# A hybrid decoder step: attention of all superblocks first, then the feed-forward over three equal segments by seven-product (Strassen) multiplication

## The chip, the cores and the metric

The kernel runs on one core of a Trainium2 chip. A core has five engines that run side by side and wait for each other by semaphores: TensorE (PE, matrix products; its weight loads are shown apart as PEld), VectorE (DVE), ScalarE (ACT), GpSimd (POOL) and SyncE (SP), which here only issues transfers. SBUF is the on-chip memory of 128 partitions, PSUM the accumulators of PE in eight banks of 512 columns, DRAM the memory outside. The metric is the device time of one launch in microseconds (us); less is better.

## The reference

One layer of a decoder is computed for 2048 prompt tokens and for 64 sample tokens (8 sequences of 8), with weights in common, in float32. For the prompt:

```
h = rmsnorm(x) * g_mix;  q, k, v, u = split(h @ w_in)          # 1024 -> 512, 128, 128, 512
a = window attention(q, k, v)      # 8 heads, window 128, ALiBi, one sink a head
p = pooling mixer(u)               # means over 2, 4, 8, 16 tokens minus u, @ w_pool, * pool_scale
x = x + concat(a, p) @ w_out
h = rmsnorm(x) * g_cross;  s = (h @ w_cq) . mem_k
x = x + (softmax(s / 16) @ mem_v) @ w_co                       # 4 heads, 256 memory tokens
h = rmsnorm(x) * g_ffn
x = x + relu(h @ w_up)**2 @ w_down                             # 1024 -> 4096 -> 1024
y = rmsnorm(x) * g_final
```

The sample tokens go the same way with caches of keys, values, pooling inputs and memory. The outputs are y, the last keys, values and pooling inputs of both groups, and the memory's keys and values.

## The kernel before, in words

**Number format.** Every large product is made of three: each operand is split in a rounded part "hi" (ACT casts) and the rest "lo" (DVE subtracts), and PE adds hi x hi, hi x lo and lo x hi (`mm3`, lines 111 to 113, and `dense`, lines 280 to 282). Weights are split too: `Stream.emit` takes two slots of `WS` (12 slots of 128x1024) and one raw buffer of `FS` (6), loads 512 KB (L131), casts (L132) and subtracts (L133). `Stream.items` is a fixed list in the order of use; `pump` runs ahead as long as slots and raw buffers are free and fewer than five tiles are ready, with `resW` and `resF` keeping some back.

**Order of work.** The tokens lie in three superblocks of two blocks each (384 + 384, 384 + 384, 256 + 320 with the sample tokens). A prologue computes the memory's keys and values and folds them with w_cq and w_co into the matrices `a_s` and `b_s` in DRAM; w_pool is folded into the lower half of w_out (`wo_s`). Then `superblock(s)` runs all stages of one superblock before the next one begins:

- input projection (10 chunks of 128 output columns by 2 blocks) mixed with the window attention, whose scratch lies in the buffers `XT` of x;
- output stage: 8 chunks by 2 blocks; each result is added to x in `XT` (`add_evac`, L884), squared and summed for the norm (`Norm.sq`, L205 and L206);
- cross stage: two halves of two heads; each half takes four tiles of `a_s` at once and goes over the 128-token tiles of both blocks (24 matmuls of 512 columns a tile);
- B stage: 8 chunks of `b_s` by 2 blocks (`add_evac2`, L1085), then the norm and the split into the feed-forward's input `h3` (`Norm.apply`, L232, 233 and 235);
- feed-forward: eight groups of 512 hidden columns. `up(g)` makes four chunks by two blocks of 24 matmuls; `up_evac` does relu on ACT, the square on POOL (L1123), the cast on ACT (L1125) and the rest on DVE (L1126). `down(g - 1)` makes 4 tiles by 2 blocks by 2 halves of 12 matmuls, each added to x by DVE (L1156). The next superblock's x is loaded and normed (`norm1`) beside the last two down groups; `final` makes the final norm and stores y.

**What sets the order of the queues.** The program is unrolled, tiles carry their dependences, and a scheduler puts the instructions of each engine in an order at build time; each engine then works through its queue in that order. `later` and `flush` hold generators that emit deferred work (norms) between chunks. All transfers are issued by SP.

Each weight of the feed-forward is loaded and split once a superblock, three times in all.

## Time and profile before

| what | us |
|---|---|
| median of 3 runs (2638.29 to 2641.51) | 2640.59 |
| profiled execution: listed by its span | 2639.7 |
| PE busy | 2565.7 |
| DVE busy | 1302.4 |
| ACT busy | 984.2 |
| POOL busy | 680.7 |
| splits of weights on DVE (L133, 330 of them) | 422.8 |
| casts of weights on ACT (L132, 330 of them) | 346.9 |

The page gives the profiled execution's span, from its first to its last instruction; no other time of that execution is listed, and the span stands 0.9 us under the median of the runs. A line that starts with L and a number is that line of the kernel. In rows of groups, "out<-in" names the tiles with their numbers left out (`w` weight slots, `f` raw buffers, `mm` and `aux` PSUM, `act` activations, `t` scratch, `x` the residual), then come the count, the busy time, the mean duration, and the idle time of the engine just before them with what ended it. In stretches of the span each engine has its busy time and its count of instructions; the last three columns are the clock granted to PE as a share of full speed, the busy share of the 16 DMA engines, and GB/s. Durations of neighbouring matmuls overlap, so their cost is the distance of their starts.

### The profile page before, as it was taken

To read this page: it belongs to the slowest core of one execution; us is meant where nothing else is said; L and a number is where in the kernel's file an instruction comes from. 1 tells how busy PE (TensorE), PEld (TensorE's weight loads), DVE (VectorE), ACT (ScalarE), POOL (GpSimd) and SP (SyncE) were. 2 spreads that over 40 slices of the span, in tenths; PEclk is the share of its full clock that TensorE was granted. 3 is DMA by queue.
4 is the path that set the end of the run, shared out by engine and by line. 5 is a ranking of instruction groups with operands and counts; after the bars stand their busy time and mean duration, and the time that the engine had idled before them with its cause. 6 is when DMAs were issued, how large, how long until landed. Compare 5 with 4: busy or idle time off the path is not lost. (4 is left out here: it accounts for less than half of the span.)

```text
span 2639.7 us, 39195 instructions
## 1 busy us (share of the span) xinstructions
PE 2565.7 (97%) x15725; PEld 2458.0 (93%) x15725; DVE 1302.4 (49%) x2276; ACT 984.2 (37%) x1923; POOL 680.7 (26%) x730
## 2 busy tenths in 40 slices
PE   7899999999999999999999999999999999999998
PEld 7798979999999999997999999999999669999998
DVE  7568453633333357936363333334766646334334
ACT  6666342422222244834342222223355434332231
POOL 3215322411111153433241111113334214111111
PEclk9999999999999999999999999999999999999999
DMA  7843212211111123131111111112414473222210
GB/s 261 260 130 101 72 49 74 71 64 63 61 62 64 56 72 113 45 132 56 65 58 63 65 64 64 65 56 71 140 60 149 176 266 112 87 80 81 88 57 37
DMA packets 92251, 244.76 MB, mean 93 GB/s; under 512 B 16740, under 2 KB 31524, under 8 KB 90916
## 3 DMA queue, kind: packets, MB, share of 16 engines
q1 hardware_dynamic: 92068, 242.25, 26.9%
q8 instruction: 123, 2.02, 0.3%
q14 instruction: 60, 0.49, 0.1%
HBM read 219.53 MB, written 22.69 MB: 92 GB/s over the span
## 5 line engine op out<-in xcount | busy, mean ns | idle before, releaser
L281 PE MATMUL mm<-act,w 128*128 128x384 f32 (+2 forms) x2784 | 899.1, 323 | 6.5 <-DVE act L235 5.0
L280 PE MATMUL mm<-act,w 128*128 128x384 f32 (+2 forms) x2784 | 902.8, 324 | 2.5 <-ACT act L623 1.6
L282 PE MATMUL mm<-act,w 128*128 128x384 f32 (+2 forms) x2784 | 897.4, 322 | 1.1 <-DVE w L133 0.9
L132 ACT CAST w<-f 128x1024 fp32r<-128x1024 f32 x330 | 346.9, 1052 | 737.4 <-PE mm L112 453.9
L133 DVE TENSOR_TENSOR w<-f,w 128x1024 fp32r<-128x1024 f32 x330 | 422.8, 1286 | 317.9 <-ACT w L132 312.0
L111 PE MATMUL mm<-act,w 128*128 128x384 f32 (+2 forms) x1728 | 554.1, 321 | 13.6 <-ACT act L372 8.3
L112 PE MATMUL mm<-act,w 128*128 128x384 f32 (+2 forms) x1728 | 550.3, 318 | 0.0
L113 PE MATMUL mm<-act,w 128*128 128x384 f32 (+2 forms) x1728 | 549.8, 318 | 0.0
L281 PEld LDWEIGHTS mm<-act,w 128*128 128x128 f32 x2784 | 527.3, 189 | 16.3 <-DVE act L235 6.7
L280 PEld LDWEIGHTS mm<-act,w 128*128 128x128 f32 x2784 | 527.4, 189 | 7.2 <-issue 2.3
L282 PEld LDWEIGHTS mm<-act,w 128*128 128x128 f32 x2784 | 527.3, 189 | 1.8 <-DVE w L133 1.6
L1123 POOL TENSOR_TENSOR t<-t 128x384 f32<-128x384 f32 (+2 forms) x192 | 219.0, 1141 | 1034.8 <-ACT t L1122 1034.8
L1156 DVE TENSOR_TENSOR x<-mm,x 128x384 f32<-128x384 f32 (+2 forms) x384 | 199.7, 523 | 326.5 <-PE mm L113 326.5
L111 PEld LDWEIGHTS mm<-act,w 128*128 128x128 f32 x1728 | 328.6, 190 | 15.8 <-ACT act L372 8.3
L112 PEld LDWEIGHTS mm<-act,w 128*128 128x128 f32 x1728 | 328.3, 190 | 1.2 <-DVE act L373 0.2
L113 PEld LDWEIGHTS mm<-act,w 128*128 128x128 f32 x1728 | 328.4, 190 | 0.1
L206 POOL TENSOR_TENSOR t<-t,t 128x384 f32<-128x384 f32 (+2 forms) x168 | 203.0, 1209 | 348.9 <-ACT t L205 331.4
L1126 DVE TENSOR_TENSOR act<-t,act 128x384 fp32r<-128x384 f32 (+2 forms) x192 | 103.2, 537 | 300.4 <-ACT act L1125 300.4
L1125 ACT CAST act<-t 128x384 fp32r<-128x384 f32 (+2 forms) x192 | 93.8, 488 | 237.5 <-POOL t L1123 237.5
L1122 ACT ACTIVATE t<-mm 128x384 f32<-128x384 f32 (+2 forms) x192 | 88.2, 459 | 95.2 <-PE mm L282 94.2
L205 ACT ACTIVATE t<-x 128x384 f32<-128x384 f32 (+2 forms) x140 | 68.4, 499 | 145.4 <-DVE x L1085 64.9
L111 PE MATMUL mm<-w,act 128*128 128x512 f32 x288 | 116.7, 406 | 3.2 <-ACT f L330 1.7
(184 smaller groups left out, 2199.0 us busy)
## 6 DMA issues: line engine op xcount, KB each, us to landing
f<-in_wup SPq DMA_DIRECT2D x96, 512.0 KB, 3.5
f<-in_wdn SPq DMA_DIRECT2D x96, 512.0 KB, 3.5
f<-in_win SPq DMA_DIRECT2D x30, 512.0 KB, 3.6
f<-a_s SPq DMA_DIRECT2D x24, 512.0 KB, 3.2
f<-b_s SPq DMA_DIRECT2D x24, 512.0 KB, 4.2
x<-in_x SPq DMA_DIRECT2D x6, 1536.0 KB, 7.1
f<-in_wco SPq DMA_DIRECT2D x16, 512.0 KB, 4.9
f<-in_cmk SPq DMA_DIRECT2D x16, 512.0 KB, 4.5
```

Source lines behind the costliest of these rows:

```text
L111: nc.tensor.matmul(ps, Wh(k), Hh(k), start=first and i == 0, stop=False)
L112: nc.tensor.matmul(ps, Wh(k), Hl(k), start=False, stop=False)
L113: nc.tensor.matmul(ps, Wl(k), Hh(k), start=False, stop=final and i == last)
L132: nc.scalar.copy(th[:], r[:, 0:1024])
L133: eng.tensor_tensor(tl[:], r[:, 0:1024], f32(th[:]), ALU.subtract)
L206: nc.gpsimd.tensor_tensor(self.acc[:, 0:n], self.acc[:, 0:n], t[:, 0:n], ALU.add)
L280: nc.tensor.matmul(ps[:, 0:n], w8(th)[:, k, :], hi(b, k), start=k == 0, stop=False)
L281: nc.tensor.matmul(ps[:, 0:n], w8(th)[:, k, :], lo(b, k), start=False, stop=False)
L282: nc.tensor.matmul(ps[:, 0:n], w8(tl)[:, k, :], hi(b, k), start=False, stop=k == 7)
L1123: nc.gpsimd.tensor_tensor(q[:, 0:n], r[:, 0:n], r[:, 0:n], ALU.mult)
L1126: nc.vector.tensor_tensor(lo, q[:, 0:n], f32(hi), ALU.subtract)
L1156: nc.vector.tensor_tensor(bl.x(m), ps[:, 0:n], bl.x(m), ALU.add)
```

## The change

**Order.** `superblock(s)` now ends with the B stage. The residual x goes to `xq` and the normed input of the feed-forward to `hq`, both in DRAM. The next superblock's norm is loaded and squared in the second half of the cross stage, and applied in the B stage. After the third superblock, `mlp` goes over all 2112 tokens in three segments of 704, each with a left and a right half of 352 columns.

**Products.** A group of up has its weight (1024 x 512) in 2 x 2 blocks and the input in 2 x 2 blocks; instead of eight block products seven are made, in a form of Strassen's scheme. The seven combinations of the input are made once a segment (`xprep`, POOL sums, ACT casts, DVE subtractions), 14 slots of `ACTS`. The results are combined when they are emptied from PSUM (`ups`). Down groups 0 to 6 do the same (`downs`), with the input's combinations made from the hidden values in place (`hsplit`, two pairs of slots in turn), and with the outputs accumulated in combined form in x and in two extra accumulators, which `mid` undoes in the last of them. Down group 7 stays plain (`down_last`), and so does the final norm.

**Weight sums.** The combinations of the weights are made once, by `Work`: 60 jobs of load, five sums of 128x256 on DVE, store to `us_s` or `ds_s`; one step of it is run after each output chunk and each cross tile (`prep`), with two buffers in turn. The untouched block of each group is copied within DRAM, as are w_in, the upper half of w_out and the last group of w_down.

**Buffers.** `WS` has 10 slots instead of 12, but the window attention's keys (4 slots) move to a new shared tile "mc". Weights that were stored by the kernel, and w_in and w_out from superblock 1 on, are loaded straight into their lo slot; only `ext` items have a raw buffer. PSUM is grouped in four tiles of two banks for `mlp`.

The host's side lays x out by superblock and reads y by segment. The core of the diff:

```diff
         def emit(self):
-            key, raw, eng = self.items.popleft()
+            key, raw, eng, ext = self.items.popleft()
             th, tl = WS.get(), WS.get()
-            r = FS.get()
+            r = FS.get() if ext else f32(tl[:])
...
     for s in range(3):
         for c in CIN:
-            S.add(("in", s, c), io["win"][c])
+            S.add(("in", s, c), win_s[c] if s else io["win"][c], ext=s == 0)
...
+    for j in range(NSEG):
         for g in range(9):
...
+            if g < 8:
+                for i in ORD:
+                    S.add(("us", j, g, i), us_s[g, WIX[i]])
+            if 0 < g < 8:
+                for i in ORD:
+                    S.add(("ds", j, g - 1, i), ds_s[g - 1, WIX[i]], eng=nc.gpsimd if i in (5, 1) else None)
+            if g == 8:
+                for c in range(4):
+                    S.add(("dn", j, c), dn_s[c])
...
-        kz = [[WS.get() for _ in range(2)] for _ in range(2)]
+        kzt = mc_tile(F32R)
+        kz = [[kzt[:, 896 * (2 * kv + hl):896 * (2 * kv + hl) + 896] for hl in range(2)] for kv in range(2)]
...
             nc.vector.tensor_tensor(bl.x(c), ps[:, 0:bl.n], bl.x(c), ALU.add)
             bl.norm.sq(c)
+            prep(s)
...
                         flush()
+                        prep(s)
+                        if hf == 1 and nxt is not None:
+                            x = len(sqs)
+                            for k in range(4):
+                                if x + k < 16:
+                                    nxt[(x + k) // 8].nm.sq((x + k) % 8)
+                                    sqs.append(1)
...
+        def after_co(b):
+            bl = blks[b]
+            for hf in range(2):
+                ACTS.put(*bl.pt[hf])
+            keep(xq, bl)
+            bl.norm.fin()
+            yield
+            for k in range(8):
+                nc.vector.scalar_tensor_tensor(bl.x(k), bl.x(k), vec[:, V_GFFN + k:V_GFFN + k + 1], bl.norm.r[:, 0:bl.n], ALU.mult, ALU.mult)
+                if k % 4 == 3:
+                    yield
+            TS.put(bl.norm.r)
+            keep(hq, bl)
...
+        def ups(j, g):
+            c11, c12, c21, c22 = Rv(g, 0, 0), Rv(g, 1, 0), Rv(g, 0, 1), Rv(g, 1, 1)
+            sm = {}
+            for i in ORD:
+                th, tl = S.next(("us", j, g, i))
+                while i not in Xc:
+                    flush()
+                Hh, Hl = Xc[i]
+                d = DD.get()
+                for q in range(2):
+                    mm3(d[:, 512 * q:512 * q + nh], range(4), lambda k: th[:, 512 * q + P * k:512 * q + P * k + P], lambda k: tl[:, 512 * q + P * k:512 * q + P * k + P],
+                        lambda k: Hh[:, nh * k:nh * k + nh], lambda k: Hl[:, nh * k:nh * k + nh])
+                WS.put(th, tl)
+                v = v2(d)
+                if i in (2, 5):
+                    t = sm[i] = TD.get()
+                    nc.scalar.copy(w2(t), v)
+                if i == 4:
+                    nc.vector.tensor_tensor(c21, v, w2(sm[2]), ALU.add)
+                    sm[4] = d
+                    relu2(c21)
...
+        def hsplit(g, i, dst):
+            X11, X21, X12, X22 = R(g, 0, 0, 2), R(g, 0, 2, 2), R(g, 1, 0, 2), R(g, 1, 2, 2)
+            pre = {4: (X21, X11, ALU.subtract), 3: (X12, X22, ALU.subtract), 1: (X11, X22, ALU.add),
+                   7: (X21, X11, ALU.add), 6: (X12, X11, ALU.add)}.get(i)
+            if pre:
+                nc.gpsimd.tensor_tensor(pre[0], pre[0], pre[1], pre[2])
+            src = {2: X11, 5: X22, 4: X21, 3: X12, 1: X11, 7: X21, 6: X12}[i]
+            hi, lo = dst[:, 0:2 * nh], dst[:, 2 * nh:4 * nh]
+            nc.scalar.copy(hi, src)
+            nc.vector.tensor_tensor(lo, src, f32(hi), ALU.subtract)
+            return hi, lo
...
+            make(0)
+            make(1)
+            for x, i in enumerate(ORD):
+                th, tl = S.next(("ds", j, g, i))
+                Hh, Hl = hc[x]
+                for pp in range(2):
+                    d = DD.get()
+                    for q in range(2):
+                        p = 2 * pp + q
+                        mm3(d[:, 512 * q:512 * q + nh], range(2), lambda k: th[:, 256 * p + P * k:256 * p + P * k + P], lambda k: tl[:, 256 * p + P * k:256 * p + P * k + P],
+                            lambda k: Hh[:, nh * k:nh * k + nh], lambda k: Hl[:, nh * k:nh * k + nh])
+                    if i in (4, 5):
+                        if g == 0:
+                            nc.scalar.copy(mac(i, pp), v2(d))
+                        else:
+                            nc.vector.tensor_tensor(mac(i, pp), v2(d), mac(i, pp), ALU.add)
+                    else:
+                        for e in (7, 6) if i == 1 else (i,):
+                            r = role(*M[e], pp)
+                            nc.vector.tensor_tensor(r, v2(d), r, ALU.add)
+                    DD.put(d)
+                    flush()
+                WS.put(th, tl)
+                if mid is not None:
+                    mid(i)
+                make(x + 2)
...
+        def step(self, load=True):
+            done = self.summed
+            self.summed = []
+            for x, t in self.loaded:
+                self.sums(t)
+                self.summed.append((x, t))
+            self.loaded = []
+            for x, t in done:
+                self.store(x, t)
+                self.bufs.append(t)
+            if load and self.jobs and self.bufs:
+                x, t = self.jobs.pop(0), self.bufs.pop(0)
+                self.load(x, t)
+                self.loaded.append((x, t))
...
+        def sums(self, t):
+            b = [t[:, 256 * i:256 * i + 256] for i in range(6)]
+            for d, a, c, op in ((4, 2, 3, ALU.add), (5, 0, 1, ALU.add), (2, 2, 0, ALU.subtract), (1, 1, 3, ALU.subtract), (0, 0, 3, ALU.add)):
+                nc.vector.tensor_tensor(b[d], b[a], b[c], op)
```

581 lines of the change are left out of this document (441 added, 140 removed).

## The prediction

> **What bounds the kernel now.** The page comes first. Its header and its line of busy time:
>
> ```profile
> span 2639.7 us, 39195 instructions
> ...
> PE 2565.7 (97%) x15725; PEld 2458.0 (93%) x15725; DVE 1302.4 (49%) x2276; ACT 984.2 (37%) x1923; POOL 680.7 (26%) x730
> ```
>
> PE has work 97% of the span, and 74.0 us are idle. Busy time alone doesn't show that PE is at its peak, so I next read the busy time by stretches: the start, the output stage and the cross stage of superblock 0, a stretch of its feed-forward, and the feed-forward of superblock 2.
>
> ```profile
> core 0: us, PE busy (x) PEld busy (x) DVE busy (x) ACT busy (x) POOL busy (x), PEclk, DMA share, GB/s
> 0.00:17.00 17.00, 8.27 (x50) 7.83 (x50) 7.54 (x15) 11.58 (x22) 4.76 (x10) 1.00 0.84 309
> 240.00:312.00 72.00, 70.01 (x392) 68.83 (x391) 28.02 (x38) 22.60 (x36) 28.41 (x28) 0.98 0.36 125
> 312.00:385.00 73.00, 69.82 (x329) 57.38 (x328) 45.88 (x75) 31.62 (x74) 23.81 (x29) 1.00 0.16 51
> 600.00:800.00 200.00, 200.00 (x1156) 200.00 (x1155) 68.90 (x96) 48.49 (x73) 27.69 (x24) 1.00 0.19 64
> 2240.00:2610.00 370.00, 370.00 (x2769) 370.00 (x2768) 145.22 (x231) 103.56 (x175) 62.77 (x61) 1.00 0.21 72
> ```
>
> In the feed-forward PE never pauses and DVE is busy 34% of the time (68.90 of 200). So the time of this part is the number of matmuls by the spacing of their starts. The timeline of PE gives the spacing for 384, 256 and 320 columns (the rows are three matmuls apart):
>
> ```profile
> 800.30 0.33 PE L280 MATMUL mm<-act,w 128*128 128x384 f32 x1
> ...
> 800.82 0.33 PE L280 MATMUL mm<-act,w 128*128 128x384 f32 x1
> ```
> ```profile
> 2299.90 0.28 PE L280 MATMUL mm<-act,w 128*128 128x256 f32 x1
> ...
> 2300.26 0.31 PE L280 MATMUL mm<-act,w 128*128 128x320 f32 x1
> ...
> 2300.70 0.31 PE L280 MATMUL mm<-act,w 128*128 128x320 f32 x1
> ```
>
> 0.52/3 = 0.1733 us, 0.36/3 = 0.1200 us and 0.44/3 = 0.1467 us. Halfway between 320 and 384 columns lies the new width of 352: 0.1600 us.
>
> **The matmuls removed.** Before, up and down take 32 tiles x 24 matmuls each, per block: 3072 of 384 columns in each of superblocks 0 and 1 (532.5 us each), and 1536 of 256 and 1536 of 320 columns in superblock 2 (409.6 us): 1474.5 us. After, a segment has 8 up groups of 7 products of 24 matmuls, 7 down groups of the same, and a plain last group of 2 x 4 x 24: 1344 + 1176 + 192 = 2712. Three segments are 8136 matmuls, 1301.8 us. **PE: -172.7 us.** All of it lies where PE sets the end, so it is gained in full if the seven products can be fed and emptied.
>
> The Trainium skill, "TensorE: Matmul & The Clock Gate", section Back-to-back issue gap, gives N/2.4 + 2.5 ns for an isolated matmul, by which the saving would be 160.8 us, an estimate; this trace has 173 ns at 384 columns where that formula has 162.5, and the rows above stay in the sum.
>
> **Weights without a raw buffer.** The six raw buffers of the stream go; a stored tile is now loaded straight into its "lo" slot. So its transfer can't start before PE has let go of the slot, and transfer, cast and split stand in a row behind that.
>
> ```profile
> f<-a_s SPq DMA_DIRECT2D x24, 512.0 KB, 3.2
> f<-b_s SPq DMA_DIRECT2D x24, 512.0 KB, 4.2
> ```
> ```profile
> L132 ACT CAST w<-f 128x1024 fp32r<-128x1024 f32 x330 | 346.9, 1052 | 737.4 <-PE mm L112 453.9 <-PE mm L281 237.5 <-issue 8.1
> L1125 ACT CAST act<-t 128x384 fp32r<-128x384 f32 x128 | 65.9, 515 | 164.0 <-POOL t L1123 164.0
> ```
> ```profile
> L133 DVE TENSOR_TENSOR w<-f,w 128x1024 fp32r<-128x1024 f32 x330 | 422.8, 1286 | 317.9 <-ACT w L132 312.0 <-PE mm L113 5.5
> L1156 DVE TENSOR_TENSOR x<-mm,x 128x384 f32<-128x384 f32 x256 | 141.5, 556 | 233.6 <-PE mm L113 233.6
> L1126 DVE TENSOR_TENSOR act<-t,act 128x384 fp32r<-128x384 f32 x128 | 73.1, 571 | 230.3 <-ACT act L1125 230.3
> ...
> L1156 DVE TENSOR_TENSOR x<-mm,x 128x256 f32<-128x256 f32 x64 | 26.8, 421 | 15.4 <-PE mm L113 15.4
> ```
>
> In the feed-forward five pairs of slots put a load four products (4 x 24 x 0.16 = 15.4 us) ahead of its use; 3.5 + 1.05 + 1.29 = 5.9 us fit, the 3.5 lying between the two rows. But the cross stage holds four pairs at once: when it turns to its second half, one tile is ready and the second is needed six matmuls later. Cross matmuls have 512 columns:
>
> ```profile
> 376.19 0.39 PE L111 MATMUL mm<-w,act 128*128 128x512 f32 x1
> ...
> 376.87 0.39 PE L111 MATMUL mm<-w,act 128*128 128x512 f32 x1
> ```
>
> 0.68/3 = 0.227, so 1.4 us later, against 3.2 + 1.05 + 1.29 = 5.5: 4.2 us of stall. At the start of B the second tile is needed after 24 x 0.173 = 4.2 us and comes after 6.5: 2.4 us. **+20 us** for three superblocks; between 0 (the scheduler finds other matmuls) and 40 (transfers slowed by the next point).
>
> **Weight sums in the output and cross stages.** 60 jobs, one for each output chunk or cross tile: 28 in superblock 0, 28 in 1, 4 in 2. Each loads 0.52 MB, makes five sums of 128x256 on DVE (0.45 us each, above the 421 ns row, which has the same width) and stores 0.79 MB. DVE: 28 x 2.25 = 63 us beside the 28.0 + 45.9 of 145 us in the two rows above: 94% full, and in the cross stage alone 45.9 + 12 x 2.25 = 72.9 of 73.0, so that any pause there is late. DMA: superblock 0 moves 28 x 1.31 + 9.4 of whole copies + 7 x 0.52 of untouched blocks + its own 12.7 (125 x 72 + 51 x 73) = 62 MB; at 309/0.84 = 368 GB/s this is 169 us for 145. Who queues behind it is seen in the waits of the DMA queue:
>
> ```profile
> SPq L131 <- DVE w L133: 1622.3, 228, 30.9
> ```
>
> SP stands at the head of its queue for a slot most of the time, so a store that waits for its sums holds up the loads behind it, and a sum on DVE that waits for its load holds up the evictions behind it. What bounds this: each of two buffers goes through load (4.2), sums (2.25) and store (1.5 x 4.2): 12.75 us, a job each 6.4 us; 28 jobs take 178 us against 16 x 4.16 + 12 x 5.44 = 132, 46 us late, 92 for two superblocks. Against that, the order of a queue isn't the program's: the stream emits all of in_woa ahead of a_s, and SP issued
>
> ```profile
> 234.98 0.32 SPq L131 DMA_DIRECT2D f<-a_s  x1
> 240.17 0.33 SPq L131 DMA_DIRECT2D f<-in_woa  x1
> ```
>
> so the scheduler puts what is ready ahead; and four PSUM tiles give PE 16 us of lead. **+25 us**, between 0 and 92, nearer the low end.
>
> **Feeding and emptying the products.** PE spends 7 x 24 x 0.16 = 26.9 us on an up group and as much on a down group. Two rows show what an operation costs when DVE runs on without a pause, and what POOL does to it:
>
> ```profile
> 961.12 2.04 DVE L133 TENSOR_TENSOR w<-f,w 128x1024 fp32r<-128x1024 f32 x1
> 963.08 1.47 DVE L1156 TENSOR_TENSOR x<-mm,x 128x384 f32<-128x384 f32 x3
> 965.14 1.23 DVE L133 TENSOR_TENSOR w<-f,w 128x1024 fp32r<-128x1024 f32 x1 [0.58 <-ACT w L132]
> ```
> ```profile
> 962.15 5.09 POOL L206 TENSOR_TENSOR t<-t,t 128x384 f32<-128x384 f32 x3
> ```
>
> While POOL works, the split with both inputs in SBUF takes 2.04 instead of 1.23 us, but evictions from PSUM go on at 0.49 each. At 704 columns I add 320 x (556 - 421)/128 ns = 0.34: 0.83 us. Down group: 16 evictions 13.3, 7 "lo" halves 5.8, 6 weight splits of 1.23 (the seventh is POOL's) 7.4: 26.5 of 26.9 us. Up group: 8 x 0.83 + 7.4 = 14.0. ACT at 0.515 x 704/384 = 0.94 stays under 20 us in either. So DVE turns from 34% to full in the down groups. POOL's operand sums are 1.278 x 704/384 = 2.34 us each:
>
> ```profile
> L206 POOL TENSOR_TENSOR t<-t,t 128x384 f32<-128x384 f32 x112 | 143.1, 1278 | 218.6 <-ACT t L205 202.4 <-DVE t L380 12.0 <-ACT t L202 2.0
> ```
>
> Two of five have their inputs early and can run in the up group before; three, 7.0 us, fall among DVE's work, half of which (13.2 of 26.5) has both inputs in SBUF: 3.5 us. 30.0 - 26.9 = 3.1; of this 2.0 is carried over, since an operand is due one product (3.84) after its buffer is free and takes 0.94 + 0.83. 1.1 us by 21 groups: **+24 us**, from 0 to the last rival's 185.
>
> **Edges of segments.** In the last Strassen group and the plain group (57.6 us of PE) DVE gets 26.5 + 3.3 for merging + 11.6 for splitting the next segment's operands + 34 for plain evictions, splits and the final norm: 75, of which the next up group takes up 10: 8 us late, twice, and about 4 at the entry from superblock 2: **+20**, from 0 to 40. The products' weights are hidden as long as DMA is nearly free there: 327 weight tiles instead of 192, 171 MB in 1302 us or 132 GB/s, where the row at 600 us has 64 GB/s for a share of 0.19. The residual and the normalised x now go out to DRAM before the next superblock may use their buffer; eight multiplies and 1.5 MB (4 us at 368 GB/s) lie under eight leading chunks of 24 x 0.173 = 33 us, and without that cover would cost some 10. The next superblock's first norm moves from the feed-forward into the cross and B stages with its loads, squares and POOL additions; its 16 multiplies have B's 66 us as cover, and cost up to 10 if that is full, within the 20.
>
> **Sum.** -172.7 + 20 + 25 + 24 + 20 = -83.7. The profiled execution is listed by its span alone, 2639.7, which is 0.9 below the median of 2640.59 of the runs; 2639.7 - 83.7 + 0.9 = **2557 us**.
>
> **Rivals.** *All is hidden but the weight waits* (chance 0.16): 2640.6 - 172.7 + 20 = 2488. For it: an up group leaves DVE 26.9 - 14.0 = 12.9 us free, enough for every delay of a down group if the buffers reached that far, and the stores may trail into later stages; against it: DVE at 26.5 of 26.9, and the two full stages. *The stored sums set the pace of the output and cross stages* (0.10): 92 instead of 25, 2624. For it: 62 MB; against: the reordering. *DVE and POOL shut each other out, and the down groups become theirs* (0.12, slower): all five operand sums and two POOL splits of 3.4 us, 18.5 us, fall on DVE's work in the proportion of one half, 9.2, and nothing is carried: 26.5 + 9.2 - 26.9 = 8.8 by 21 = 185 in place of 24, so 2718. It decides from 5.1 us a group, which is (172.7 - 65)/21. For it: 2.04 against 1.23; against: evictions pass, and POOL has idle up groups. The Trainium skill, "SBUF — State Buffer", section Who interferes with whom, states it as an exclusive lock for a whole instruction between a DVE operation with two SBUF inputs and a POOL operation that reads SBUF; the rows above agree, and by that rule this rival is as likely as POOL's placement makes it.
>
> **Numbers.** The forecast has 0.62. The range, 2480 to 2635, takes in the first and the third way, with the bounds of the four costs as far as they go together, and leaves out the slower one. A measurement here tells some 0.2% (5 us) from no change: faster 0.88, within it 0.02, slower 0.10.
>
> **What would show it.** Matmuls of 352 columns should start 0.160 us apart; up groups should have no PE idle time and down groups a little behind DVE "lo" halves; PE's waits should name the weight split in the cross stage. I am wrong if PE's waits there total over 70 us, if down groups take over 32 us, or if matmuls are spaced otherwise.

## The result, and the profile after

The changed kernel takes 2962.24 us (median of 4 runs, 2953.5 to 2962.72) against 2640.94 for the kernel before beside it: ratio 1.121, 95% interval 1.120 to 1.123. It is slower by 321 us, where 2557 was forecast and no case reached above 2718. Line numbers from here on are those of the changed kernel (mm3 is L147 to L149, the weights' load, cast and split L167 to L169, the output stage's eviction L945, the sums of a job L1634, its store L1639), unless another kernel is named.

The page of the changed kernel, its header, busy times, and the rows of PE and of the granted clock:

```profile
span 2960.9 us, 38618 instructions
...
PE 2525.7 (85%) x14655; PEld 2352.0 (79%) x14655; DVE 1941.6 (66%) x2822; ACT 1265.7 (43%) x2055; POOL 854.1 (29%) x707
...
PE   6888835689895883888979999969999989999997
...
PEclk8999967789997986999989999989999999999998
```

PE has 1070 matmuls fewer, and 435 us of idle time instead of 74. The holes lie in the first half, before the feed-forward, and in two spots within it, about 1925 and 2425 us. Busy time by stretches shows where: the output and cross stages of superblock 0 (300 to 575), its B stage (575 to 680), steady groups of the feed-forward (1535 to 1900) and the first edge between two segments.

```profile
core 0: us, PE busy (x) PEld busy (x) DVE busy (x) ACT busy (x) POOL busy (x), PEclk, DMA share, GB/s
300.00:410.00 110.00, 72.96 (x385) 68.72 (x383) 32.88 (x57) 18.10 (x32) 24.03 (x22) 0.84 0.45 155
410.00:466.00 56.00, 17.75 (x38) 11.76 (x39) 26.58 (x49) 8.72 (x13) 4.73 (x4) 0.56 0.60 203
466.00:575.00 109.00, 73.34 (x309) 55.65 (x309) 51.60 (x103) 31.04 (x81) 25.98 (x38) 0.84 0.61 204
575.00:680.00 105.00, 80.60 (x402) 75.19 (x401) 59.45 (x98) 30.98 (x50) 24.88 (x27) 0.87 0.44 150
1535.00:1900.00 365.00, 361.08 (x2209) 357.75 (x2210) 272.50 (x283) 184.58 (x213) 101.29 (x50) 0.99 0.43 144
1925.00:1975.00 50.00, 30.41 (x149) 27.99 (x147) 48.44 (x38) 19.99 (x25) 33.48 (x15) 0.82 0.31 103
```

The prediction read these two stages of the kernel before from 240 to 385 us. They lie some 20 us later: the first eviction of the output stage is at 270.6 and the last cross matmul at 397.8. The stretches that fit them, in the same columns:

```profile
264.00:332.00 68.00, 66.01 (x364) 62.93 (x363) 31.71 (x41) 20.63 (x34) 23.69 (x18) 1.00 0.21 74
332.00:402.00 70.00, 68.81 (x329) 57.12 (x328) 37.91 (x70) 30.99 (x77) 15.44 (x26) 1.00 0.18 59
```

So what took 138 us before now takes 275 (300 to 575), and no engine and no queue is full over it: DVE 111 of 275, DMA at 0.45 to 0.61. The feed-forward's steady groups run as forecast, with PE busy for 361 of 365 us.

To add this up I take each distance between the starts of two neighbouring matmuls, subtract what full speed needs, (columns + 32)/2400 us (0.1733 at 384, 0.1600 at 352, 0.227 at 512, the spacings of the prediction), and split what is left over: the idle time that the profile shows before a matmul counts as idle, the rest as slow spacing:

| | matmuls at full speed | idle | slow spacing |
|---|---|---|---|
| before | 2490.5 | 55.9 | 75.2 |
| after | 2320.0 | 415.8 | 206.0 |
| difference | -170.5 | +359.9 | +130.8 |

So the forecast gain of 172.7 is there: the products of the feed-forward need 172.8 us less by their count, and the other matmuls 2.2 more. On top come 491 us of idle time and slow spacing. The waits of PE name the weights first:

```profile
PE mm L147 <- ACT w L168: 90.6, 7, 22.4
PE mm L324 <- ACT w L168: 45.9, 6, 22.2
PE mm L324 <- DVE mc L577: 44.7, 2, 44.4
```

and the waits of SP's queue name what held up their loads (us in total, times, longest). Only two rows are larger, 594.7 and 579.7, weight loads that wait for a slot which a product still reads:

```profile
SPq L1639 <- DVE mc L1634: 283.8, 21, 51.5
```

The timelines of SP and of DVE in the output stage of superblock 0 show one such wait in full:

```profile
312.88 1.22 SPq L1639 DMA_DIRECT2D us_s<-mc  x1
314.14 3.17 SPq L1641 DMA_DIRECT2D win_s<-in_win  x1
323.24 1.20 SPq L1626 DMA_DIRECT2D mc<-in_wup  x2
362.88 0.37 SPq L1639 DMA_DIRECT2D us_s<-mc  x1
...
375.15 0.43 SPq L167 DMA_DIRECT2D fb<-in_woa  x1
```
```profile
355.39 0.56 DVE L945 TENSOR_TENSOR x<-mm,x 128x384 f32<-128x384 f32 x1 [3.61 <-PE mm L326]
360.50 0.56 DVE L945 TENSOR_TENSOR x<-mm,x 128x384 f32<-128x384 f32 x1 [4.55 <-PE mm L326]
360.97 3.68 DVE L1634 TENSOR_TENSOR mc<-mc 128x256 f32<-128x256 f32 x10
```

SP issues the load of a job (two transfers) at 323 and then stands at a store until 362.88: 38 us. The store waits for the sums at 360.97, and those stand on DVE behind the evictions of fourteen chunks. Behind the store wait the loads of w_out, the next of them issued at 375.15; PE finishes the last chunk for which it has weights at 360.1 and idles for 22 us. The three queues were tied in a ring: weights behind a store, the store behind sums, the sums behind evictions, the evictions behind PE, PE behind weights.

### The profile page after: what moved, and what is told of

It is laid out like the page before. It is cut to its first block, busy times and chain, and to the rows that moved or that the text cites. A ratio compares the mean times of both kernels' runs of the same rounds, so it can differ in the third digit from the quotient of the medians.

```text
span 2960.9 us, 38618 instructions
## 1 busy us (share of the span) xinstructions
PE 2525.7 (85%) x14655; PEld 2352.0 (79%) x14655; DVE 1941.6 (66%) x2822; ACT 1265.7 (43%) x2055; POOL 854.1 (29%) x707
## 4 chain that ended last, share of the span: by engine, by line
PE 59%; DVE 17%; DMA 8%; issue 6%; ACT 6%; POOL 4%; SPq 1%; DVEq 0%; POOLq 0%; ACTq 0%
PE mm L147 8%; PE mm L148 8%; PE mm L149 8%; PE aux L148 6%; PE aux L149 6%; PE aux L147 6%; PE mm L324 5%; PE mm L326 4%; PE mm L325 4%; DVE w L169 3%; DVE x L1408 2%; DVE ts L276 2%; POOL ts L250 2%; DMA ds_s<-mc 1%; DVE mc L1634 1%
## 5 line engine op out<-in xcount | busy, mean ns | idle before, releaser
L168 ACT CAST w<-w 128x1024 fp32r<-128x1024 f32 x411 | 430.9, 1052 | 671.0 <-DMA w<-us_s 286.0
L169 DVE TENSOR_TENSOR w<-w,w 128x1024 fp32r<-128x1024 f32 x369 | 489.2, 1328 | 137.6 <-ACT w L168 136.6
L324 PE MATMUL mm<-act,w 128*128 128x384 f32 (+2 forms) x1248 | 428.7, 344 | 147.6 <-ACT w L168 45.9
L326 PE MATMUL mm<-act,w 128*128 128x384 f32 (+2 forms) x1248 | 414.6, 335 | 6.6 <-DVE w L169 6.5
L325 PE MATMUL mm<-act,w 128*128 128x384 f32 (+2 forms) x1248 | 416.6, 334 | 2.1 <-DVE act L688 2.1
L324 PEld LDWEIGHTS mm<-act,w 128*128 128x128 f32 x1248 | 250.0, 200 | 168.1 <-ACT w L168 48.1
L147 PE MATMUL mm<-act,w 128*128 128x352 f32 (+1 forms) x1092 | 354.0, 325 | 22.5 <-ACT act L417 8.5
L148 PE MATMUL mm<-act,w 128*128 128x352 f32 (+1 forms) x1092 | 349.6, 320 | 6.2 <-DVE act L1377 6.1
L149 PE MATMUL mm<-act,w 128*128 128x352 f32 (+1 forms) x1092 | 349.7, 321 | 0.0
L1373 POOL TENSOR_TENSOR fb<-fb 128x704 f32<-128x704 f32 x105 | 213.3, 2032 | 438.2 <-DVE ar L1377 264.3
L148 PE MATMUL aux<-act,w 128*128 128x352 f32 x932 | 302.9, 325 | 10.4 <-DVE act L1504 7.0
L147 PE MATMUL aux<-act,w 128*128 128x352 f32 x932 | 303.7, 326 | 7.6 <-ACT act L1503 6.0
L149 PE MATMUL aux<-act,w 128*128 128x352 f32 x932 | 303.6, 326 | 2.5 <-DVE w L169 2.5
L326 PEld LDWEIGHTS mm<-act,w 128*128 128x128 f32 x1248 | 247.4, 199 | 11.7 <-DVE w L169 9.3
L325 PEld LDWEIGHTS mm<-act,w 128*128 128x128 f32 x1248 | 248.9, 200 | 4.2 <-DVE act L688 2.4
L250 POOL TENSOR_TENSOR ts<-ts 128x384 f32<-128x384 f32 (+2 forms) x133 | 145.9, 1098 | 368.5 <-ACT ts L249 365.3
L147 PEld LDWEIGHTS mm<-act,w 128*128 128x128 f32 x1092 | 211.4, 194 | 27.0 <-ACT act L417 8.4
L148 PEld LDWEIGHTS mm<-act,w 128*128 128x128 f32 x1092 | 212.2, 194 | 9.1 <-DVE act L1377 7.8
L147 PE MATMUL mm<-w,act 128*128 128x512 f32 x288 | 124.4, 441 | 105.8 <-ACT w L168 90.6
L149 PEld LDWEIGHTS mm<-act,w 128*128 128x128 f32 x1092 | 211.3, 194 | 0.3 <-DVE w L169 0.2
L1634 DVE TENSOR_TENSOR mc<-mc 128x256 f32<-128x256 f32 x300 | 135.7, 502 | 93.8 <-DMA mc<-in_wup 59.5
L148 PEld LDWEIGHTS aux<-act,w 128*128 128x128 f32 x932 | 177.7, 191 | 13.5 <-DVE act L1504 7.9
```

Of the source, the lines that this page charges most:

```text
L147: nc.tensor.matmul(ps, Wh(k), Hh(k), start=first and i == 0, stop=False)
L148: nc.tensor.matmul(ps, Wh(k), Hl(k), start=False, stop=False)
L149: nc.tensor.matmul(ps, Wl(k), Hh(k), start=False, stop=final and i == last)
L168: nc.scalar.copy(th[:], r[:, 0:1024])
L169: eng.tensor_tensor(tl[:], r[:, 0:1024], f32(th[:]), ALU.subtract)
L250: nc.gpsimd.tensor_tensor(self.acc[:, 0:n], self.acc[:, 0:n], t[:, 0:n], ALU.add)
```

## Theories

A: this ring, made by the order of the queues, is the loss. B: weights without a raw buffer come too late. C: the transfers are too many. Later, when these left half of the loss open, D: PSUM slots that are halves of two-bank tiles; and E: at the edges, DVE and POOL shut each other out. Each experiment below is a single run unless an interval is given; the kernel before stood at 2640 to 2642 beside all of them. Kernels that ran several times spread by up to 10 us, so a difference of two single runs below that says nothing.

## Experiments on the changed kernel

**No jobs** (`e1_no_jobs`). The products of the feed-forward read tiles of `a_s` and `b_s` instead of stored sums; the whole copies stay, one behind each chunk, and the copies of untouched blocks go with the jobs.

```diff
-                    S.add(("us", j, g, i), us_s[g, WIX[i]])
+                    S.add(("us", j, g, i), b_s[WIX[i]])
...
-                self.jobs += [("u", g, j) for j in range(4)]
-                if g < 7:
-                    self.jobs += [("d", g, j) for j in range(4)]
+                pass
...
```

> Leaves out the 60 jobs of weight sums (loads, sums, stores and the copies of untouched blocks); the seven products take tiles of a_s and b_s as weights, the seven whole copies stay. Theory A, queue orders: a store at the head of SP's queue waits for sums that stand behind evictions in DVE's, and the weight loads stand behind the store. Then nearly all of the 392 us that PE lost ahead of the feed-forward beyond the kernel before comes back, about 60 stay: 2630 us. Theory C, too many bytes: the same, 2630. Theory B, weights without a raw buffer come late: little changes, over 2850.

Measured 2728. The jobs cost 234 us, which speaks against B. But A and C both expected 2630, and neither had the kernel without its jobs still 87 us slower than before. Two questions were left: what in the jobs, and what besides them.

**Jobs without sums** (`e5_no_dve_sums`): the same transfers, the five sums left out, so a store waits for its load alone.

```diff
...
-            for d, a, c, op in (...):
-                nc.vector.tensor_tensor(b[d], b[a], b[c], op)
+            pass
```

> Leaves out the five sums of each job, so that a store waits for its load alone; all transfers stay as they are in number and size (the third part of each buffer is zero). Theory A: the tie between SP and DVE is gone, most of the loss comes back, about 2700 us. Theory B and theory C: nothing changes but DVE's work, over 2880.

2853: between both. Without the tie to DVE 109 us come back, and 125 stay with the transfers and their order.

**Weights issued by ACT** (`e3_stream_act_queue`), so that they no longer stand behind SP's stores.

```diff
-                nc.sync.dma_start(r[:, w * i:w * i + w], src)
+                nc.scalar.dma_start(r[:, w * i:w * i + w], src)
```

> The weight stream's loads are issued from ACT's queue, the jobs' transfers stay in SP's. Theory A: weights no longer stand behind stores that wait for sums; what PE waited for casts ahead of the feed-forward (137 us, with the slow clock after them some 190) comes back, and the 44 us of superblock 2 stay: about 2770 us. Theory B and theory C: no change, 2930 to 2990.

3070, slower by 108. The output and cross stages became clean (PE idle 5.5 and 2.8 us in superblock 0), but with nothing to hurry them the jobs ran into the next attention, whose keys need the same tile `mc`. The waits of PE in this kernel:

```profile
PE mm L324 <- DVE mc L577: 118.3, 2, 113.7
PE aux L732 <- ACT mc L576: 109.1, 2, 108.7
```

Cutting the ring at one place moved the wait to the next holder of the buffer.

**Stores not kept in program order** (`e4_unpinned`).

```diff
-            tc.keep_in_program_order(nc.sync.dma_start(dst, ...))
+            nc.sync.dma_start(dst, ...)
...
```

(and so for the copies behind them.)

> The stores and copies of the jobs are no longer held in program order on SP; all else is the same. If this pin makes the bad order (one form of theory A), the time falls below 2880 us. If the order comes from the scheduler's own view of what is ready, or theories B or C hold, it stays within 2930 to 2990.

2970: nothing beyond the spread. The kept order of the stores isn't what puts the sums so late.

**Half of the jobs** (`e6_half_jobs`), at half the rate.

```diff
-    RATE = 1.0
+    RATE = 0.5
...
```

> The changed kernel with 30 of its 60 jobs, one at every second output chunk or cross tile; the products of the other groups read a_s and b_s tiles, so the output differs. Without jobs it took 2728, with all 2962. Theory of pace (two buffers give a job each 6.4 us, wanted each 4.2 to 5.4): at half the rate a job has 8.3 us or more, so nearly nothing is late: 2728 to 2760. Theory of the tied queues (every store stands on SP behind sums that stand on DVE behind evictions): every job costs the same, half of 234 is left: 2830 to 2860. Theory of bytes: in proportion too, about 2845, but the waits would be on transfers and not on SP's stores.

2866: 138 of 234 remain. That is a price per job, and not that of a pace which two buffers can't hold; the 46 us a superblock by which the prediction bounded this term came from the wrong mechanism. The time alone doesn't tell the ring from the bytes (2845 expected), but SP's waits do lie at the stores that wait for sums: 172.6 us in 12 waits, where the whole change has 283.8 in 21.

## What the jobs did not explain

The start and the attention stages of the kernel without jobs still lost more than before, so I put parts of the change into the kernel **before**.

**PSUM pairs alone** (`b1_psum_pairs`). The eight slots become halves of four two-bank tiles. The change needs the pairs for the feed-forward alone, but declares them for the whole program, the superblocks included.

```diff
-    MM = Slots([psp.tile([P, 512], ...) for i in range(4)])
+    PS = [psp.tile([P, 1024], ...) for n in ("mm", "aux") for i in range(2)]
+    MM = Slots([PS[i][:, 512 * q:512 * q + 512] for i in range(2) for q in range(2)])
```

> The kernel before, with its eight PSUM slots as halves of four tiles of two banks and nothing else; computes everything. Without jobs the changed kernel still lost about 40 us more than before in the start and the first attention stage and 20 to 30 more in each later attention stage. Theory that slots sharing a tile wait for each other: 2660 to 2730 here. Rival (the loss is from fewer buffers or from the copies): 2636 to 2646.

2829, ratio 1.071 (1.069 to 1.073): 187 us for three lines of declarations, in a kernel that nothing else was changed in. PE's idle time rises from 55.9 to 146.0 and its slow spacing from 75.2 to 169.8. The waits of PE for the operations that empty `mm` (six lines, L1157 the first with 17.6 us) come to 70 us, where the kernel before has 3. One place in this kernel (timelines of PE and DVE, line numbers one above those of before; L885 is the output stage's eviction):

```profile
1247.58 0.34 PE L283 MATMUL mm<-act,w 128*128 128x384 f32 x1
1254.22 0.69 PE L281 MATMUL mm<-act,w 128*128 128x384 f32 x1 [6.30 <-DVE x L885]
```
```profile
1253.61 1.02 DVE L885 TENSOR_TENSOR x<-mm,x 128x384 f32<-128x384 f32 x2 [4.94 <-DMA x<-in_x]
1260.91 0.56 DVE L885 TENSOR_TENSOR x<-mm,x 128x384 f32<-128x384 f32 x1 [6.28 <-PE mm L283]
```

The evictions wait for x from DRAM; PE stands still with two chunks not yet evicted, though there are four slots, and goes on 0.05 us after the first of the two evictions ends (1253.61 + 0.56). By the count of slots it could have run two chunks (8.3 us) further. So a half seems to come free only with its neighbour, or to wait for the neighbour's reader; which of the two the trace doesn't tell, nor how much of the 187 us comes from another order of the queues at build time.

**Weights without a raw buffer alone** (`b2_direct_ab`).

```diff
-            r = FS.get()
+            ext = key[0] not in ("A", "B")
+            r = FS.get() if ext else f32(tl[:])
```

> The kernel before, with the stored tiles of the cross and B stages loaded straight into their lo slot, without a raw buffer; computes everything. The prediction's price for this is 20 us for three superblocks (0 to 40): 2660. Theory that the direct load is what made the changed kernel slow: over 2700. Rival, the scheduler covers it: 2636 to 2648.

2643, ratio 1.0003 (0.9991 to 1.0014). So for the tiles that the prediction priced theory B is out, and its 20 us too. The direct loads of the other weights, and ten slots in place of twelve, were not tried apart.

**Six scratch buffers as slices** (`b3_six_ts`).

```diff
-    TS = Slots([sb(f"t{i}", 400) for i in range(nT)])
+    tsb = sb("ts", 400 * nT)
+    TS = Slots([tsb[:, 400 * i:400 * i + 400] for i in range(nT)])
```

> The kernel before, with six small scratch buffers that are slices of one SBUF tile in place of eight single ones; computes everything. If slices of an SBUF tile wait for each other as halves of a PSUM tile do: over 2680. If only the number counts: 2640 to 2665. If neither: 2636 to 2646.

2646, ratio 1.0022 (1.0011 to 1.0034), 5 us. What slices of a PSUM tile do, slices of this SBUF tile don't do.

## Edges of the segments

DVE and PE in the first edge of the changed kernel:

```profile
1931.98 2.35 DVE L1377 TENSOR_TENSOR act<-fb,act 128x704 fp32r<-128x704 f32 x1
...
1937.98 2.37 DVE L1377 TENSOR_TENSOR act<-fb,act 128x704 fp32r<-128x704 f32 x1
1940.27 1.69 DVE L1404 TENSOR_TENSOR mc<-mm,mc 128x704 f32<-128x704 f32 x2
...
1953.38 0.88 DVE L1377 TENSOR_TENSOR act<-fb,act 128x704 fp32r<-128x704 f32 x1
```
```profile
1934.39 0.66 PE L148 MATMUL mm<-act,w 128*128 128x352 f32 x1 [4.78 <-DVE act L1377]
```

The same "lo" half takes 2.35 us while POOL works (21.5 of the 25 us from 1925 to 1950) and 0.88 when it doesn't; evictions from PSUM stay at 0.84 to 0.88 each. This is what the prediction's rows showed at 2.04 against 1.23, and its slower rival placed it in the down groups. It sits in the edges instead, where POOL has the merges and the next segment's operand sums. The Trainium skill, "SBUF — State Buffer", section Who interferes with whom, states an exclusive lock between a DVE operation with two SBUF inputs and a POOL operation that reads SBUF; by that rule the "lo" halves wait and the evictions pass, and the rows above agree.

**These on DVE** (`e7_edge_dve`, without jobs).

```diff
-                nc.gpsimd.tensor_tensor(dst[:, c], dst[:, c], other[:, c], op)
+                nc.vector.tensor_tensor(dst[:, c], dst[:, c], other[:, c], op)
...
-                merge(2, 4, ALU.add, nc.gpsimd)
+                merge(2, 4, ALU.add, nc.vector)
```

(and so for every merge and for `adjust`.)

> The kernel without jobs (2728; the products read a_s and b_s tiles), and at the edges of segments the operand sums and the merges go from POOL to DVE, where one takes 0.88 us with nothing beside it; the computation of the edges stays whole. In the edge from 1900 to 2025 of the changed kernel POOL is busy 60 us and DVE's splits take 2.2 to 2.7 us instead of 0.88 to 1.23. Theory that DVE and POOL shut each other out there: the edges' 84 us of PE loss fall by 25 to 50, time 2680 to 2705. Rival, DVE simply has too much to do: DVE gets some 25 us more work at each edge, time 2740 to 2780. Rival, the operands come late from DRAM: no change, 2720 to 2735.

2703 against 2728: 25 us less, at the low end of E's range; giving DVE more work made the edges shorter, which speaks against a DVE that simply has too much to do. But the moved sums also became shorter, from 2.0 to 2.4 us each on POOL to 0.88 on DVE, so the run doesn't tell how much of the 25 us is the exclusion and how much a shorter chain of operand sums.

## The causes together

**Single PSUM tiles in the superblocks** (`e8_sep_psum`), pairs only in the feed-forward, which needs them.

```diff
+    sctx = ExitStack()
-    psp = ctx.enter_context(tc.tile_pool(name="ps", ...))
+    psp = sctx.enter_context(tc.tile_pool(name="ps", ...))
...
+    MM = Slots([psp.tile([P, 512], ...) for i in range(4)])
...
+    sctx.close()
+    psq = ctx.enter_context(tc.tile_pool(name="ps2", ...))
+    PS = [psq.tile([P, 1024], F32, name=f"dd{i}", tag=f"dd{i}") for i in range(4)]
     mlp(mt)
```

> The changed kernel whole, but with eight single PSUM tiles in the superblocks, as before, and the four pairs only from the feed-forward on. In the kernel before the pairs alone took the time from 2642 to 2829, about 142 us of it outside the feed-forward (matmuls of the same chunks compared). Theory that the pairs are one cause of their own beside the jobs: 2962 - 142 = 2820, between 2790 and 2840. Theory that pairs and jobs multiply (shorter lead of PE over evictions is what tied the queues): 2640 to 2760. Rival, the jobs' waits hide the pairs' waits: 2880 to 2950.

2821.4 for an expected 2820: the pairs are a cause of their own, 140.8 us. That the two agree to 1.4 us is luck, given the spread of single runs.

**And the edges on DVE** (`e10_sep_edge`):

> The same, with the operand sums and merges at the edges of segments on DVE instead of POOL; computes everything. That step was worth 25 us in the kernel without jobs (2728 to 2703): 25 below the single-tile kernel if the causes add, 2765 to 2815; nothing if the edges' wait is elsewhere once PSUM is free.

2788.3: another 33.1. This is called the repaired kernel from here on.

**And no jobs** (`e9_sep_nojobs_edge`):

> The same without the 60 jobs (the products read a_s and b_s tiles, so the output differs): 2703 - 142 = 2561 if the pairs cost here what they cost before, which is about the predicted 2557 less its 25 for the jobs; if the start and attention lose for another reason (fewer buffers, transfers): 2640 to 2690.

2597.3: 43 us under the kernel before, though not the 2561 that the sum gave. So in the repaired kernel the jobs, with the copies of untouched blocks, cost 191 us.

## What in the jobs

Four edits of the repaired kernel (2788) that should have cut the ring or eased the pace all made it slower.

`g1_pool_sums`, the sums on POOL:

```diff
-                nc.vector.tensor_tensor(b[d], b[a], b[c], op)
+                nc.gpsimd.tensor_tensor(b[d], b[a], b[c], op)
```

> The repaired kernel (single PSUM tiles, edges on DVE: 2788) with the five sums of a job on POOL instead of DVE; computes everything. Tie of the queues by DVE: the sums no longer stand behind evictions, 2640 to 2710. Pace of two buffers: the sums get slower (5 x 0.85 and more instead of 2.25 us), 2790 to 2850. Bytes: 2775 to 2800.

`g2_thru_b`, the jobs spread over the B stage too:

```diff
+            if s < 2:
+                prep(s)
...
-    RATE = 1.0
+    RATE = 0.65
```

> The repaired kernel (2788) with the jobs spread over output, cross and B stages at 0.65 of a job for each chunk or tile, sums on DVE; computes everything. Pace: a job is wanted every 6.4 to 8.3 us, as two buffers can give it: 2640 to 2700. Tie: the same number of stores waits behind evictions, 2760 to 2800. Bytes: a third thinner, 2720 to 2760.

`g3_both`, both edits:

> Both at once, computes everything: if tie and pace are the whole cost, 2600 to 2650; if bytes or the waits of POOL's other work are left, 2680 to 2760.

`g4_poolstore`, both edits and the store issued from POOL:

```diff
-            tc.keep_in_program_order(nc.sync.dma_start(dst, ...))
+            tc.keep_in_program_order(nc.gpsimd.dma_start(dst, ...))
```

> Both, and each job's store issued from POOL's queue right behind its sums, so that SP never stands at a store; computes everything. Tie of SP's queue: 2600 to 2640, below the one before by 20 to 60. If a load that waits for its buffer on SP takes the place of the store: no change against the one before.

Measured 2837, 2822, 2873 and 3104: all four of my expectations fell, A's among them. The timelines showed why a choice of engine or rate didn't help. First SP and DVE of the repaired kernel, then POOL of the kernel with POOL sums:

```profile
291.98 1.21 SPq L1626 DMA_DIRECT2D mc<-in_wup  x2
350.82 0.37 SPq L1639 DMA_DIRECT2D us_s<-mc  x1
```
```profile
319.08 0.56 DVE L945 TENSOR_TENSOR x<-mm,x 128x384 f32<-128x384 f32 x1 [3.61 <-PE mm L326]
...
347.63 0.54 DVE L279 TENSOR_TENSOR act<-ts,act 128x384 fp32r<-128x384 f32 x1
348.10 4.49 DVE L1634 TENSOR_TENSOR mc<-mc 128x256 f32<-128x256 f32 x10
360.62 1.77 DVE L1634 TENSOR_TENSOR mc<-mc 128x256 f32<-128x256 f32 x5 [8.03 <-DMA mc<-in_wdn]
```
```profile
320.49 0.99 POOL L250 TENSOR_TENSOR ts<-ts 128x384 f32<-128x384 f32 x1 [3.09 <-ACT ts L249]
321.44 7.08 POOL L1634 TENSOR_TENSOR mc<-mc 128x256 f32<-128x256 f32 x10
```

In the repaired kernel the sums stand behind the whole output stage and the norm; on POOL they stand behind a row of squares. SP waits for 58 us, and from 350 on the jobs run alone, 7.6 to 9.6 us each, with the weights of the cross stage behind them, so that PE idles for 52.6 us. Now the transfers are a limit too: in this stretch the whole copies pass between the jobs, and DMA is full (share 1.04).

```profile
360.00:390.00 30.00, 0.82 (x2) 0.50 (x2) 7.90 (x21) 1.04 (x1) 0.00 (x0) 0.50 1.04 364
```
```profile
389.18 1.22 PE L147 MATMUL mm<-w,act 128*128 128x512 f32 x2 [52.60 <-ACT w L168]
```

The order of execution, read from the traces, says the same without a clock. Here "o" is an eviction of the output stage of superblock 0 and [n] stands for the sums of n jobs:

```
changed kernel             [2]oooooooooooooo[4]oo
repaired kernel            [2]oooooooooooooooo
jobs through the B stage   [2]oooooooooooooooo
sums on POOL               [2]oooooooooooo[4]oooo
```

In the repaired kernel DVE is idle for 3.6 us before most of these evictions, and the load of the next job was issued at 291.98. Each engine works through its queue in order, so the sums had been put there at build time. What comes between the first two jobs and the third in SP's list are whole copies and untouched blocks, transfers from DRAM to DRAM behind the stores. My supposition: a scheduler that takes these for long has reason to expect the third job late and to put sixteen evictions ahead of it.

**Copies early** (`k1_early_copies`): the 22 transfers are issued in the input stage of superblock 0, everything else as in the repaired kernel.

```diff
         def in_evac(c, b, ps):
+            if s == 0 and (c, b) != (0, 0):
+                work.copy()
...
-            if self.copies:
-                tc.keep_in_program_order(nc.sync.dma_start(*self.copies.pop(0)))
-            if j == 0:
...
+        def copy(self):
+            for _ in range(2):
+                if self.copies:
+                    nc.sync.dma_start(*self.copies.pop(0))
```

> The repaired kernel (2788) with the 22 DRAM to DRAM transfers issued in the input stage of superblock 0 instead of behind the jobs' stores; sixty jobs as before, computes everything. Theory that the order is the cost (transfers listed behind the stores push the sums behind sixteen evictions): one to two sums jobs between evictions, SP's longest wait at a store under 15 us, time 2597 + the pace of two buffers, 0 to 92: 2600 to 2690. Theory of bytes (79 MB in the output and cross stages): 2750 to 2790. Rival, the transfers hurt the input stage by as much: 2780 to 2830.

(Other than that text says, this kernel and the next write the seven untouched blocks of w_down with their rows of 1 KB in another order, so that y differs; number and size of the transfers are the same.)

2680, ratio 1.015 (1.013 to 1.017): 108 of the 191 us are gone. DVE's timeline in the output stage (L947 is the eviction here, L1641 the sums) and SP's longest wait at a store:

```profile
325.91 0.55 DVE L947 TENSOR_TENSOR x<-mm,x 128x384 f32<-128x384 f32 x1
326.84 0.56 DVE L947 TENSOR_TENSOR x<-mm,x 128x384 f32<-128x384 f32 x1 [0.38 <-PE mm L326]
334.58 1.77 DVE L1641 TENSOR_TENSOR mc<-mc 128x256 f32<-128x256 f32 x5 [7.19 <-DMA mc<-in_wdn]
336.27 0.55 DVE L947 TENSOR_TENSOR x<-mm,x 128x384 f32<-128x384 f32 x1
```
```profile
SPq L1646 <- DVE mc L1641: 80.5, 25, 9.3
```

One job now stands between one or two evictions, and the longest wait is 9.3 us instead of 57.8. So the place of these transfers in the program does set the order of the sums; why the scheduler acts so isn't shown. The edit also moves their bytes out of the stretch where DMA was full: 9.4 MB of whole copies and 15 blocks of 0.52 MB are 17 MB, at 364 GB/s some 48 us (an estimate). How the 108 us divide between order and bytes was not tested; if all of the 48 us were bytes, 60 are left for the order.

**And spread, with loads and sums kept in program order** (`k4_early_pin_thru_b`):

```diff
-                nc.vector.tensor_tensor(b[d], b[a], b[c], op)
+                tc.keep_in_program_order(nc.vector.tensor_tensor(b[d], b[a], b[c], op))
...
-    RATE = 1.0
+    RATE = 0.65
```

> The same with 0.65 of a job for each chunk or tile, through the B stage, and loads and sums kept behind the eviction they follow in the program; computes everything. Theory of order plus pace: a job every 6.4 us or more fits two buffers, so 2600 to 2640, at or below the kernel before's 2640. If bytes: no change from the run beside it. If the pinned sums hold up evictions while they wait for a load: above the run beside it.

2680 again. PE's idle time in the output, cross and B stages of superblocks 0 and 1 is some 40 us, as it is in the kernel without jobs (there 27 of them in the output stage of superblock 0, where its copies stand), so there the jobs cost little at last. About 50 of the remaining 83 us lie in the first 320 us, in the input stage that now carries the copies (a load of w_in takes 14.2 us to land instead of 4.7). The two runs differ in rate and in pinning and came out the same, so the pace of two buffers, the prediction's bound of 92, is hardly what is left. No version with its jobs came under the kernel before.

## Why the prediction was wrong, step by step

- **The matmuls removed**: -172.7 forecast, -170.5 found for all matmuls together. The spacing at 352 columns is 0.160 (three matmuls from 1940.87 to 1941.35), as forecast:

```profile
1940.87 0.32 PE L147 MATMUL aux<-act,w 128*128 128x352 f32 x1
...
1941.35 0.32 PE L147 MATMUL aux<-act,w 128*128 128x352 f32 x1
```

- **Weights without a raw buffer**, +20: no change in the kernel before (ratio 1.0003). The range had this end, the forecast had not.
- **Weight sums**, +25, from 0 to 92: this is the step that failed most. 191 to 234 us. I had the ring's parts (SP at the head of its queue, sums that hold up evictions), and then let it go with "so the scheduler puts what is ready ahead". That row proved that the build reorders; it didn't say towards what. It put the sums of ready jobs behind fourteen to sixteen evictions. Moving 22 transfers mended the order and took 108 us away, an unknown part of them for the moved bytes. The bound of 92 was no bound, as it took a job's own 6.4 us for the slowest thing in the chain; with the copies between them the jobs run 7.6 to 9.6 us apart even alone. That the stretches were read some 20 us early changes this term little: DVE comes to 133 of 138 us instead of 137 of 145.
- **PSUM slots as halves of pairs**: 141 us, put at nothing. The lines stand in the diff, and I read them as a new name for the same eight banks; the weight sums' "four PSUM tiles give PE 16 us of lead" rests on that. This is the second step that failed.
- **Feeding and emptying the products**, +24: the right kind, somewhat too large. Away from the edges the down groups of the changed kernel take 27.3 to 28.5 us instead of 26.9, 0.7 us over on average where 1.1 was forecast, and up groups mostly 26.9 to 27.1. In the kernel without jobs (`e9`) the steady groups lose some 16 us against full speed, and the first four groups behind superblock 2 another 7. The slower rival, DVE and POOL shutting each other out in the down groups, did not come.
- **Edges of segments**, +20: by far too small. 33 us went when the merges left POOL. Without jobs 64 more remain around the two edges and the end (`e9`), with DVE busy for 112.34 of 134 us at the first; that DVE's work is what is left there was not tested:

```profile
1556.00:1690.00 134.00, 117.89 (x692) 114.25 (x692) 112.34 (x130) 62.56 (x78) 22.21 (x11) 0.95 0.45 151
```

The balance, from 2640.9, with the causes taken away in the order of the runs above: -170.5 for the matmuls, +140.8 pairs, +33.1 POOL at the edges, +191.0 jobs in the repaired kernel, and +126.9 for what remains without jobs, of which 78 lie in the feed-forward (its edges and steady groups, less the 10 that the feed-forward lost before) and 49 ahead of it. Together 2962.2. The +126.9 is what the sum leaves, not a measurement of its own. The last 49 weren't taken apart: copies between the output chunks may be among them (27 us of idle time in that stage of the kernel without jobs), and so may the fewer weight slots.

Of the signs that I had named, the matmul spacing came out as forecast. The down groups did so for 18 of 21; the last one of each segment, in the edges, takes 49.0, 47.4 and 40.7 us between the starts of its first matmul and the next group's, past the 32 that would make me wrong. PE's idle time in the cross stages passed its limit too: some 115 us against 70 (about 73, 37 and 5 in the three superblocks). All rivals priced one engine or one pace; none was an order of queues, and so the range had no room for it.

## What to carry to other kernels

Work hung on a stage as filler isn't priced by its duration: ask in what order the queues will hold it, and read the compiled order before trusting slack. In this kernel the place of 22 transfers that nobody waited for decided where the sums went. And a change of how buffers are declared is a step with a price: slots that share a tile may not be slots any more, which three lines put into the old kernel were enough to show.

## What the runs showed of the hardware

After these two pauses PE didn't come back at full speed. Behind the 4.78 us wait at 1934 the matmuls of 352 columns start 0.293 us apart instead of 0.160 for about 5.5 us; behind the 22.2 us wait at 382.66 those of 384 columns are 0.32 apart instead of 0.173 until 387.3 (4.6 us). The clock granted to PE is 0.50 of full speed from 363.4 to 387.3 and from 1933.5 to 1940.3, and the full spacing is back where it ends:

```profile
1934.85 0.49 PE L149 MATMUL mm<-act,w 128*128 128x352 f32 x1
1935.14 0.49 PE L147 MATMUL mm<-act,w 128*128 128x352 f32 x1
```
```profile
382.66 0.69 PE L324 MATMUL mm<-act,w 128*128 128x384 f32 x1 [22.20 <-ACT w L168]
...
384.41 0.52 PE L324 MATMUL mm<-act,w 128*128 128x384 f32 x1
384.73 0.52 PE L325 MATMUL mm<-act,w 128*128 128x384 f32 x1
```

The Trainium skill, "TensorE: Matmul & The Clock Gate", section Back-to-back issue gap, has N/1.2 ns for a matmul at the lower clock, 293 and 320 here: the trace agrees to the digit.

So the pause at 1934 costs some 2.4 us more than itself ((0.293 - 0.160) x 18 matmuls), that at 382 some 2.1 (0.147 x 14), and a stretch of short bursts runs at a granted clock of 0.56 (410 to 466). Over the whole kernel, matmuls that start while 0.5 is granted lose 105 us in spacing, against 19 before: 87 of the 131 us of slow spacing, or 18% of the 491 us of loss. The other 44 us fall at full clock, half of them right before a wait. I had priced stalls at their own length.
